# Growing the sums of seven block products in PSUM, with ScalarE copying partial sums: one step of a hybrid streaming encoder

## The chip, the core and the metric

The kernel runs on one core of a Trainium2 chip. TensorE multiplies matrices into PSUM (eight banks of 2 KB per partition), VectorE and ScalarE read PSUM and SBUF, GpSimd works in SBUF, and transfers between memory and SBUF are issued by SyncE. The metric is the device time of one launch in microseconds (us), shown as the median of three runs. In the profile PE is TensorE, PEld its loading of weights, DVE VectorE, ACT ScalarE, POOL GpSimd and SP SyncE.

## What is computed

One inference step of an encoder layer, for 4096 prompt tokens and 32 sample tokens of width 1024:

```
h    = RMSNorm_pre(x)
proj = h @ w_in      # [B_a | C_a | X_a | Z_a | qkv | Z_g | a_dec | b_beta]
y_a  = B_a * conv3_causal(C_a * X_a) * silu(Z_a)     # group A, 512 channels
y_g  = RMSNorm_head(gated_delta_rule(...)) * silu(Z_g)   # group B, 4 heads of 128
y    = x + RMSNorm_post(concat(y_a, y_g) @ w_out)
```

The outputs are y for both streams, and the last convolution inputs and recurrent states. The part that matters here is group A's four projections and the output projection.

## The kernel before, in words

Every fp32 operand of a large product is held as a pair of fp16 tiles (high and low part), and a product of two pairs takes three matmuls for each contraction tile (`mm3`, L863): high by high, high by low, low by high, over four contraction tiles, so twelve matmuls.

The kernel has three phases, which overlap at their borders. Phase 1 (up to about 1340 us of the span) works through group B in 16 blocks of 256 tokens, and prepares group A's weights beside it. Phase 2 (about 1343 to 2043 us) computes group A for eight blocks of 512 tokens; phase 3 (about 2043 us to the end) computes the output for 16 units of 256 tokens.

In phases 2 and 3 a product C = A B is computed by quarters, with seven products instead of eight (`winograd`, L869, after Strassen and Winograd). The sums of quarters of A and B are made beforehand: in `prep_a` (L659) and `h_load` (L886) for group A, in `mix_prep` (L1117) and `prep_out` (L1033) for the output. The loop over the seven products then sums their results into four quarters in SBUF, c11, c12, c21 and c22. With P0 to P6 in the order of that loop, c11 = P0 + P1, U2 = P0 + P2, U3 = U2 + P3, c12 = U2 + P4 + P5, c22 = U3 + P4, c21 = U3 + P6. The first product is copied out of PSUM by ScalarE (L877). The six others are added by VectorE to what lies in SBUF (L881): one addition for each, two for P4, so seven additions for each call.

Phase 2 calls `winograd` from `a_pairs` (L959): 64 calls, one for each block, each pair of channel tiles p = 0, 1 and each of the projections X, C, B and Z (g = 0 to 3, in this order), on quarters of 256 columns. Its seven products go two to a bank into four banks, of the tags "pj" and "g" in turn. After C, VectorE multiplies C by X (L976, two instructions of 512 columns). After Z, `conv_gate` (L944) does the causal convolution on VectorE (L946 to L951), multiplies it by B (L953), takes silu of Z on ScalarE (L955), and multiplies both on GpSimd (L957). The results of a call lie in two tiles of a ring of six (`dtile`, L857). Four calls take eight tiles, so the two tiles of Z are those of X, which the convolution uses as scratch until L953 has read them.

Beside these calls stands the preparation of the next block: `h_load` computes differences on GpSimd (L900 to L916), converts them on ScalarE (`put`, L896) and subtracts on GpSimd again (L897). `prep_out` converts w_out on ScalarE (L1053) and stores it by DMA through a ring of two tiles.

Phase 3 calls `winograd` once for each unit, from `out_unit` (L1167), on quarters of 512 columns. Each product has a bank of its own, of "pj" and "g" in turn (four banks). `norm_out` (L1145) squares the quarters on ScalarE (L1155), computes the inverse norm on VectorE (`rsqrt`, L112 to L119, and L1157 to L1160), scales on VectorE (L1163), adds the residual on GpSimd (L1164) and stores. `mix_prep` for the unit two ahead runs beside it: `token_scales` (L1087) takes absolute values on ScalarE (L1092), their sums on GpSimd (L1094) and one matmul into a bank of the tag "r" (L1089, L1095), scales the channels on VectorE (L1110), and the operands are made by ScalarE (L1128), VectorE (L1129) and GpSimd (L1135 to L1141). SBUF tiles of phase 3 come from a ring of 26 (`vtile`, L1081).

The order of instructions on each engine is not written out by hand: the framework orders them when the kernel is built, by priorities and a model of their times, so that products of neighbouring calls are interleaved. On the chip each engine runs its queue in that fixed order, and an instruction that waits holds back all behind it. A product that writes a bank waits until what was read from that bank has been read.

The banks are allotted by kind of use (L153): two each of "pj", "g" and "r", one each of "o" and "m".

Of the kernel before, what the change touches and what calls it, by code (L numbers as in the profile page):

```python
# [10 lines left out]
BF16 = mybir.dt.bfloat16  # L11
# [14 lines left out]
# Operands of the split products are scaled by powers of two: h (bounded by 32) by 2^HS, each  # L26
# column of the weights so that its sum of magnitudes lies in [2^WS, 2^(WS+1)). The sums that the
# Strassen-Winograd products take of them stay in the range of fp16, too.
# [4 lines left out]
NXT = 5  # buffers of the rows of x and of the weights in preparation  # L33
SG = 0  # the group of blocks that the sample goes with
LS = 2  # groups at the end whose products of q and k come a step earlier
XPE = 256  # tokens whose h is transposed on the tensor engine, the rest by DMA
AH = 1  # how far the preparation of weights runs ahead of the products, from step AS on
AS = 5
VLN = (20,)  # channel tiles of which the vector engine takes the scaling, or the low part
# [3 lines left out]
def bc(ap, axis, n):  # L43
    """ap with a new axis of n repeats."""
    shape = list(ap.shape)
    shape.insert(axis, n)
    return ap.unsqueeze(axis).to_broadcast(shape)
# [3 lines left out]
def hybrid_kernel(  # L51
# [24 lines left out]
    ident = const([P, P], F32, "ident")  # L76
    make_identity(nc, ident)
    tri = const([P, P], BF16, "tri")  # tri[k, i] = 1 where k <= i
# [3 lines left out]
    rev = const([P, P], BF16, "rev")  # rev[k, i] = 1 where k > i  # L82
    V.tensor_scalar(rev, tri, -1.0, 1.0, ALU.mult, ALU.add)
    # sums relative to the middle of a chunk; the last column gives its start
# [13 lines left out]
    mneg = const([P, P], F32, "mneg")  # mneg[j, i] = 0 where j <= i, else far below  # L98
# [5 lines left out]
    nea = const([P, NH], F32, "nea")  # -exp(a_log), all partitions  # L104
    dtb = const([P, NH], F32, "dtb")
    gwc = const([P, 1], F32, "gwc")
    usc = const([P, 32], F32, "usc")  # per channel tile: 1 / (scale of w * scale of h)
    ug = const([P, 8], F32, "ug")
    cw = const([P, 4, 12], F32, "cw")  # conv weights of qkv, unscaling folded in
    ca = const([P, 3, 4], F32, "ca")  # L110

    def rsqrt(x, y, t):  # L112
        """y = 1 / sqrt(x) for positive x, by Newton's iteration; t is scratch."""
# [8 lines left out]
    NB2P = SEQ // NB2  # L122
    # h of a block: (half of its rows, half of its tokens, high or low part, ...)
# [10 lines left out]
    # pairs of channel tiles of group A, in the order of their products: X, C, B, Z  # L134
    pairs = [(4 * g + 2 * p, p) for p in range(2) for g in (2, 1, 0, 3)]
    # channel tiles of group B in the order of their products
    b_order = [20, 21, 22, 23, 16, 17, 18, 19, 24, 25, 26, 27, 28, 29, 30, 31]

    def w_slot(i, shape, dtype, nm):
        """Room of 2 KB for a part of the weights."""  # L140
        return wp.tile(shape, dtype, tag=f"w{i}", name=f"w{i}_{nm}")
# [8 lines left out]
    # PSUM: the eight banks by kind of use  # L150
# [5 lines left out]
    # =================== phase 1: group B ===================  # L156
# [11 lines left out]
    def scaled(cts, n=P, urow=None):  # L168
        """Of the channel tiles of w_in (one or two): w * ln_pre with scaled columns, and the
        unscaling."""  # L170
# [4 lines left out]
        for i, ct in enumerate(cts):  # L175
            if 20 <= ct < 24:  # the first ones go to room that is not yet in use
                w = tl([P, D], F32, "v" if ct < 22 else "zg", 2, f"w{ct}")
            else:
                w = te([P, D], F32, "xt", NXT, f"w{ct}")
# [30 lines left out]
    # order of the activation tables: exponentials and silus are queued in turn  # L210
# [11 lines left out]
    def xprep(b):  # L222
        """h of the block, transposed, as an fp16 pair."""
# [8 lines left out]
        for i, t0 in enumerate(range(0, n, P)):  # L232
# [5 lines left out]
            else:  # a place that is not yet in use  # L238
# [33 lines left out]
    def gates(b):  # L272
        """Log-decays, their sums in the chunk, and the decays between its positions; by steps."""
# [26 lines left out]
        # u = 1 + e; log1p(e) = ln(u) + (e - (u - 1)) / u, sigmoid = 1 / u  # L300
# [14 lines left out]
        # the log-decays as three bf16 parts, whose sum they are  # L315
# [15 lines left out]
        # exponents: whole chunk, from here to its end, from its start to here; sum from the middle  # L331
# [22 lines left out]
    def in_turn(steps):  # L354
        """The steps of several blocks in turn."""
# [4 lines left out]
    def decays(b):  # L360
        """The decays between the positions of a chunk, and those to and from its ends."""
# [31 lines left out]
    def qkv_pair(b, c0, dst):  # L393
        """Channel tiles c0, c0+1 (of q, k, v): conv and silu into dst (P, 2, n)."""
# [20 lines left out]
    def stage1(b, c):  # L415
        """Chunk c: norms of q and k, products with k, decays."""
# [35 lines left out]
    def rnorms(b):  # L452
# [10 lines left out]
        V.tensor_tensor(br, b["beta"], rk, ALU.mult)                           # beta rk  # L463
        V.scalar_tensor_tensor(nb_, br, -1.0, rk, ALU.mult, ALU.mult)          # -b' = -beta rk^2
        V.tensor_tensor(nbe, nb_, b["e1"], ALU.mult)                           # -b' e^gb
        V.tensor_scalar(cc, rq, P ** -0.5, None, ALU.mult)                     # c = rq / sqrt(dk)
# [3 lines left out]
    def subst(b):  # L470
        """Inverses of the unit triangular 32x32 blocks on the diagonal: 32 blocks, of which lane
        (g, block) finds columns 8 g to 8 g + 7 by forward substitution."""
# [13 lines left out]
        # rows times beta / (|k|^2 + eps); |k|^2 is the block's diagonal  # L486
# [25 lines left out]
    # the inverse's transpose, for two chunks; its lower blocks stay zero  # L512
# [772 lines left out]
```

## Time and profile before

| what | value |
|---|---|
| median of 3 runs | 2450.47 us (2447.03 to 2458.69) |
| profiled execution, span | 2457.2 us |
| time around the span | not told by a view; the longest run, 2458.69 us, is 1.5 us above the span |
| busy shares over the span: PE, DVE, ACT, POOL | 88%, 77%, 43%, 53% |
| mean granted TensorE clock | 0.944 of 2.4 GHz |

The shares are means over three phases with different limits, so the rows below are taken by phase: a stretch of 583 us of phase 2 (1460 to 2043 us, where the border to phase 1 is past), and phase 3 (2043 to 2457 us). A row of a group gives the line, engine and operation, what is written and read, the shape, the count, and then the busy time and the mean duration of one; behind the second bar stands the idle time of the engine before these instructions, and what ended it.

### The profile page before, as it was taken

What the parts mean: (1) busy time and instruction counts of PE and PEld (TensorE: products, weight loads), DVE (VectorE), ACT (ScalarE), POOL (GpSimd) and SP (SyncE); (2) the same over time, 40 slices, a digit from 0 to 9 for tenths busy, and PEclk for the clock granted to TensorE, in tenths of its full rate; (3) what the DMA queues carried; (4) which work ended last, traced back from release to release, by engine and by line L of the source; (5) the groups of instructions that cost most, each with busy time, mean ns of one, the idle gap of its engine ahead of it and who ended that gap; (6) DMA issues with size and microseconds to landing.
All of it is one profiled execution on the core that took longest, in us unless ns stands there. A gap on an engine that the chain in (4) does not pass through costs nothing. (4 is left out here: it accounts for less than half of the span.)

```text
span 2457.2 us, 48833 instructions
## 1 busy us (share of the span) xinstructions
PE 2157.5 (88%) x18434; PEld 1704.9 (69%) x18434; DVE 1893.4 (77%) x4878; ACT 1046.3 (43%) x2617; POOL 1312.7 (53%) x1665
## 2 busy tenths in 40 slices
PE   3677999999999989999998799899989999888876
PEld 2565877778778777778877588787878885333332
DVE  3886879887678988668776766667684578899998
ACT  3454556555656556555653222122211133343432
POOL 3526356554464764175453724756754435556764
PEclk9888999999999999999988899999999999999988
DMA  5244343423423443233344042121121053233332
GB/s 113 53 102 92 78 94 88 113 70 85 128 73 85 111 96 110 48 100 78 68 125 148 14 175 98 50 99 57 61 82 53 10 190 107 92 116 116 121 124 86
DMA packets 301524, 227.69 MB, mean 93 GB/s; under 512 B 166904, under 2 KB 237368, under 8 KB 301288
## 3 DMA queue, kind: packets, MB, share of 16 engines
q1 hardware_dynamic: 301288, 224.58, 33.3%
q8 instruction: 144, 2.36, 0.4%
q14 instruction: 92, 0.75, 0.1%
HBM read 130.99 MB, written 77.79 MB: 85 GB/s over the span
## 5 line engine op out<-in xcount | busy, mean ns | idle before, releaser
L388 PE MATMUL pj_c<-hhi,w 128*128 128x256 f16 x1536 | 429.0, 279 | 1.2 <-DMA hhi<-xth 1.2
L390 PE MATMUL pj_c<-hhi,w 128*128 128x256 f16 x1536 | 428.8, 279 | 0.0
L389 PE MATMUL pj_c<-hlo,w 128*128 128x256 f16 x1536 | 428.7, 279 | 0.0
L867 PEld LDWEIGHTS <-w_a 128*128 128x128 f16 x2880 | 272.8, 100 | 65.7 <-issue 29.6
L495 POOL TENSOR_TENSOR la<-la,lt 128x1024 f32<-128x1024 f32 x16 | 38.7, 2421 | 459.2 <-DVE lt L490 274.8
L867 PEld LDWEIGHTS <-opm 128*128 128x128 f16 x1344 | 135.5, 102 | 212.1 <-issue 72.8
L500 POOL TENSOR_TENSOR lt<-lt 128x112 f32<-128x112 f32 (+29 forms) x496 | 251.0, 506 | 38.8
L390 PEld LDWEIGHTS <-w 128*128 128x128 f16 x2176 | 216.1, 101 | 59.8 <-POOL w L652 28.8
L499 POOL TENSOR_TENSOR lt<-la,lt 128x112 f32<-128x112 f32 (+29 forms) x496 | 231.8, 467 | 38.8
L388 PEld LDWEIGHTS <-w 128*128 128x128 f16 x2176 | 216.3, 101 | 34.7 <-issue 2.1
L389 PEld LDWEIGHTS <-w 128*128 128x128 f16 x2176 | 216.3, 101 | 31.1 <-issue 0.3
L405 DVE SCALAR_TENSOR_TENSOR qk<-u,cw,qk 128x256 f32<-128x256 f32 x384 | 215.0, 596 | 8.6 <-ACT qk L403 7.8
L867 PE MATMUL pja<-op,w_a 128*128 128x256 f16 x1536 | 197.2, 279 | 7.3 <-DVE w L881 4.1
L867 PE MATMUL pjo<-w_o,opm 128*128 128x512 f16 x672 | 170.4, 406 | 27.6 <-DVE v5c L881 5.2
L867 PE MATMUL go<-w_o,opm 128*128 128x512 f16 x672 | 162.4, 391 | 13.1 <-DVE v18c L881 2.8
L867 PE MATMUL ga<-op,w_a 128*128 128x256 f16 x1152 | 152.0, 278 | 15.3 <-DVE w L881 8.2
L388 PE MATMUL pj_z<-hhi,w 128*128 128x256 f16 x512 | 146.8, 287 | 0.0
L390 PE MATMUL pj_z<-hhi,w 128*128 128x256 f16 x512 | 146.7, 287 | 0.0
L389 PE MATMUL pj_z<-hlo,w 128*128 128x256 f16 x512 | 146.7, 287 | 0.0
L1094 POOL TENSOR_TENSOR mab<-mab 128x1024 bf16<-128x1024 bf16 (+2 forms) x48 | 82.1, 1711 | 73.2 <-ACT mab L1092 71.5
L1129 DVE TENSOR_TENSOR opm<-mx,opm 128x512 f16<-128x512 f32 x112 | 111.6, 1016 | 8.2 <-ACT opm L1128 8.2
L881 DVE TENSOR_TENSOR w<-pja,w 128x256 f32<-128x256 f32 x168 | 67.2, 419 | 59.9 <-PE pja L867 57.4
(849 smaller groups left out, 5264.2 us busy)
## 6 DMA issues: line engine op xcount, KB each, us to landing
xt<-in_x_prompt_dram SPq DMA_DIRECT2D x32, 512.0 KB
op<-hTd SPq DMA_DIRECT2D x32, 512.0 KB
mx<-mxd SPq DMA_DIRECT2D x16, 1024.0 KB
xtw<-in_w_in_dram SPq DMA_DIRECT2D x28, 512.0 KB
wad<-hl SPq DMA_DIRECT2D x56, 256.0 KB
gB<-gd SPq DMA_DIRECT2D x16, 516.0 KB
hTd<-hhi SPq DMA_DIRECT2D x16, 512.0 KB
hTd<-hlo SPq DMA_DIRECT2D x16, 512.0 KB
```

Of the source, the lines that this page charges most:

```text
L388: T.matmul(pt[:, i, :n], wh[:, k, :], b["hi"][:, k, :n], start=k == 0, stop=False)
L389: T.matmul(pt[:, i, :n], wh[:, k, :], b["lo"][:, k, :n], start=False, stop=False)
L390: T.matmul(pt[:, i, :n], wl[:, k, :], b["hi"][:, k, :n], start=False, stop=k == KT - 1)
L405: V.scalar_tensor_tensor(d, u[:, i, j:j + n], cw[:, j, c0 + i:c0 + i + 1], d, ALU.mult, ALU.add)
L495: E.tensor_tensor(la, la, bc(rl, 1, 32), ALU.mult)
L499: E.tensor_tensor(tm, bc(la[:, j, j + 1:32], 2, w), bc(lt[:, j, 0:w], 1, r), ALU.mult)
L500: last = E.tensor_tensor(lt[:, j + 1:32, 0:w], lt[:, j + 1:32, 0:w], tm, ALU.subtract)
L867: T.matmul(out, lt(x, k), rh(y, k), start=start and k == n == 0, stop=stop and k == 3 and n == 2)
L881: V.tensor_tensor(dst, p, src, ALU.add)
L1094: G.tensor_tensor(ab[:, 0:m], ab[:, 0:m], ab[:, m:2 * m], ALU.add)
L1129: V.tensor_tensor(mo[:, q, 1], src, mo[:, q, 0], ALU.subtract)
```

## The change

The seven sums grow in three PSUM banks X, Y and Z (tags "pj", "g" and "r"). The products are reordered so that X holds, one after the other, P0, then U2, then U3, then c21, by matmuls that add to what is there. Y holds one product, and Z the sum of two. ScalarE copies a bank's partial sum to SBUF at each point where it is needed. VectorE keeps two additions from PSUM (c11 and c12). One more addition, of two SBUF tiles (c22), is given to VectorE in group A and to GpSimd in the output. The last sum, c21, stays in PSUM for the caller: the C projection multiplies it from there, the others copy it on ScalarE. The order of operands follows the new order of products. `token_scales` takes its bank from the tag "m" in place of "r". Comments are removed throughout, which is left out here.

```diff
-    def mm3(out, lt, rh, start, stop):
+    def mm3(out, lt, rh, start, stop, more=False):
         for k in range(4):
             for n, (x, y) in enumerate(((0, 0), (0, 1), (1, 0))):
-                T.matmul(out, lt(x, k), rh(y, k), start=start and k == n == 0, stop=stop and k == 3 and n == 2)
+                T.matmul(out, lt(x, k), rh(y, k), start=start and k == n == 0, stop=stop and k == 3 and n == 2,
+                         skip_group_check=more)
-    def winograd(lts, rhs, ps, c11, c12, c21, c22):
-        for i, p in enumerate(ps):
-            mm3(p, lts[i], rhs[i], True, True)
-            if i == 0:
-                A.activation(c21, p, AF.Copy)
-            else:
-                for dst, src in (((c11, c21),), ((c12, c21),), ((c21, c12),), ((c12, c12), (c22, c21)),
-                                 ((c12, c12),), ((c21, c21),))[i - 1]:
-                    V.tensor_tensor(dst, p, src, ALU.add)
+    def winograd(lts, rhs, nm, n, c11, c12, u3, c22, E):
+        X, Y, Z = (bank(t, [P, n], f"{t}{nm}") for t in ("pj", "g", "r"))
+        def p(i, b, start):
+            mm3(b, lts[i], rhs[i], start, True, not start)
+        p(0, X, True)
+        A.activation(c11, X, AF.Copy)
+        p(1, Y, True)
+        V.tensor_tensor(c11, Y, c11, ALU.add)
+        p(2, X, False)
+        A.activation(c12, X, AF.Copy)
+        p(3, Z, True)
+        A.activation(c22, Z, AF.Copy)
+        p(4, X, False)
+        A.activation(u3, X, AF.Copy)
+        E.tensor_tensor(c22, c22, u3, ALU.add)
+        p(5, Z, False)
+        V.tensor_tensor(c12, Z, c12, ALU.add)
+        p(6, X, False)
+        return X
...
     def a_pairs(j, op, p):
...
-            ps = [bank("pgpg"[i] + "j" * (i % 2 == 0), [P, 2, NB1], f"a{nm}_{i}") for i in range(4)]
...
-            winograd([lambda x, k, q=q: w[q][:, x, k] for q in (0, 1, 4, 5, 3, 6, 2)],
-                     [lambda x, k, q=q: op[:, q, x, k] for q in (0, 2, 5, 4, 1, 3, 6)],
-                     [ps[i // 2][:, i % 2] for i in range(7)], ds[0][:, l], ds[0][:, h], ds[1][:, l], ds[1][:, h])
+            c21 = winograd([lambda x, k, q=q: w[q][:, x, k] for q in (0, 1, 4, 3, 5, 6, 2)],
+                           [lambda x, k, q=q: op[:, q, x, k] for q in (0, 2, 5, 1, 4, 3, 6)],
+                           f"a{nm}", NB1, ds[0][:, l], ds[0][:, h], ds[1][:, l], ds[1][:, h], V)
             got.append(ds)
             if g == 1:
-                for i in range(2):
-                    V.tensor_tensor(ds[i], ds[i], got[0][i], ALU.mult)
+                V.tensor_tensor(ds[1][:, l], c21, got[0][1][:, l], ALU.mult)
+                V.tensor_tensor(ds[0], ds[0], got[0][0], ALU.mult)
+                V.tensor_tensor(ds[1][:, h], ds[1][:, h], got[0][1][:, h], ALU.mult)
+            else:
+                A.activation(ds[1][:, l], c21, AF.Copy)
...
     def token_scales(nm, mx, n):
-        ap_ = bank("r", [P, NB1], f"am{nm}")[:, :n]
+        ap_ = bank("m", [P, NB1], f"am{nm}")[:, :n]
...
     def out_unit(u):
...
-        ps = [bank(("pj", "g")[(u + i) % 2], [P, 512], f"o{u}_{i}") for i in range(7)]
-        winograd([lambda x, k, q=q: mo[:, q, x, k] for q in range(7)],
-                 [lambda x, k, q=q: WO[q, k][:, x] for q in range(7)], ps, c11, c12, c21, c22)
+        order = (0, 1, 2, 4, 3, 5, 6)
+        x = winograd([lambda x, k, q=q: mo[:, q, x, k] for q in order],
+                     [lambda x, k, q=q: WO[q, k][:, x] for q in order], f"o{u}", 512, c11, c12, vtile(f"u3{u}"), c22, G)
+        A.activation(c21, x, AF.Copy)
```

## Rows read from the trace of the kernel before

**Rows 1.** Busy time by stretch: us, PE, PEld, DVE, ACT, POOL; clock, DMA share, GB/s.

```profile
1460.00:2043.00 583.00, 543.38 (x4955) 476.43 (x4954) 383.89 (x752) 119.86 (x236) 316.43 (x249) 0.98 0.25 86
2043.00:2457.00 414.00, 339.32 (x1472) 151.25 (x1469) 382.33 (x705) 158.13 (x346) 253.00 (x159) 0.92 0.34 109
...
1840.00:1880.00 40.00, 40.00 (x369) 35.85 (x367) 21.34 (x49) 5.66 (x11) 19.32 (x17) 1.00 0.04 14
```

**Rows 2.** What TensorE waited for, 1460 to 2043 us: total, times, longest.

```profile
PE ga L867 <- DVE d L881: 10.5, 4, 3.3
PE ga L867 <- DVE w L881: 8.5, 5, 2.9
PE pja L867 <- DVE w L881: 8.1, 10, 2.3
PE pja L867 <- DVE d L881: 5.4, 10, 1.5
PE pja L867 <- ACT w L877: 4.3, 2, 3.8
```

**Rows 3.** The chain that ended last, 2200 to 2260 us: start, us, what.

```profile
2225.74 2.53 DVE v21c L1163
...
2229.93 0.61 DVE v3c L881
2230.59 4.35 PE pjo L867 x12
```

**Rows 4.** VectorE's additions L881 alone, by stretch: us, DVE, clock, DMA share, GB/s.

```profile
1460.00:2043.00 583.00, 159.16 (x394) 0.98 0.25 86
2043.00:2457.00 414.00, 76.03 (x117) 0.92 0.34 109
```

**Rows 5.** ScalarE's copies L877: group, and one of phase 3 (timeline).

```profile
L877 ACT ACTIVATE w<-pja x38: 360/383/384, 1465.6 to 2037.6; 128x256 f32<-128x256 f32 x38
...
2231.35 0.58 ACT L877 ACTIVATE v11c<-go 128x512 f32<-128x512 f32 x1
```

**Rows 6.** Timeline, 2216 to 2230 us: start, us, instruction, idle time before.

```profile
2216.39 2.75 PE L867 MATMUL pjo<-w_o,opm 128*128 128x512 f16 x12
...
2218.98 2.75 PE L867 MATMUL go<-w_o,opm 128*128 128x512 f16 x12
...
2223.32 0.74 DVE L1163 SCALAR_TENSOR_TENSOR v19c<-v19c,oss,v26lnq 128x512 f32<-128x512 f32 x1
2223.48 1.71 POOL L1164 TENSOR_TENSOR v24x<-v20c,v24x 128x512 f32<-128x512 f32 x1 [2.14 <-DVE v20c L1163]
...
2223.98 1.76 DVE L1163 SCALAR_TENSOR_TENSOR v22c<-v22c,oss,v27lnq 128x512 f32<-128x512 f32 x1
...
2229.86 0.68 DVE L881 TENSOR_TENSOR v3c<-pjo,v3c 128x512 f32<-128x512 f32 x1
```

**Rows 7.** ScalarE's copies L877, 1460 to 2043 us: idle until (us, times).

```profile
  PE pja L867: 132.1, 30
  DVE w L953: 46.2, 7
  DVE d L953: 22.7, 5
```

**Rows 8.** What ScalarE waited for, 1460 to 2043 us.

```profile
ACT op L896 <- POOL tsc L902: 80.8, 22, 6.3
ACT op L896 <- POOL tsc L913: 38.0, 10, 4.1
ACT hl L1053 <- DMA wod<-hl: 36.5, 16, 5.8
...
ACT op L896 <- POOL tsc L916: 22.7, 9, 4.5
```

**Rows 9.** Clock beside a long stall, and beside short ones: us, PE, clock, DMA.

```profile
2229.00:2235.00 6.00, 4.41 (x13) 0.72 0.09 22
...
1640.00:1680.00 40.00, 37.77 (x344) 1.00 0.20 67
```

## The prediction

> **What bounds the kernel now.** The page gives TensorE 88% of the span and VectorE 77%, but these are means over phases, so I first read busy time by stretch. In phase 2 (583 us) TensorE issues 4955 matmuls. In a stretch where it is never idle, 369 of them take 40 us, 0.108 us each [rows 1], so the 4955 need 537 us and 46 us are lost. In phase 3 (414 us) VectorE is busy for 382 us, 92%, and TensorE for 339 [rows 1]. A product of twelve matmuls there takes 2.59 us from start to start [rows 6], so the seven of a unit take 18.1 us, and 16 units 290 us. So phase 2 is bound by TensorE with some holes, and phase 3 by VectorE.
>
> Next, what opens the holes. In phase 2 the waits of TensorE name VectorE's additions L881 four times, 10.5 + 8.5 + 8.1 + 5.4 = 32.5 us, and ScalarE's copy with 4.3 us [rows 2]. The rest of the 46 us are short gaps and time at a lower clock. In phase 3 the chain of waits goes along VectorE from one operation to the next and reaches TensorE only through an addition [rows 3]: the product that starts at 2230.59 us was released by an addition that stood in VectorE's queue behind a scaling. That product took 4.35 us where the earlier ones started 2.59 us apart [rows 3, 6], and the granted clock around it was 0.72 [rows 9]. So a long stall costs twice: the idle time, and a slower product after it.
>
> **The change, part by part.**
>
> *VectorE's additions, phase 3.* A unit goes from seven additions from PSUM to two, so 16 x 5 = 80 leave. In the chain such an addition takes 0.61 us from its start to the next step [rows 3], with 0.68 us of its own [rows 6]. At 0.60, 80 of them are 48 us. VectorE sets the end here, so this counts in full at first. Bounds: 0 if another engine takes over at once, 48 if none does.
>
> *The sum c22 on GpSimd, phase 3.* This is 16 additions of two SBUF tiles. The nearest row of that shape takes 1.71 us [rows 6], so 27 us on GpSimd, which goes from 253 to 280 us of 414 [rows 1]; it stays free enough. But the same scaling on VectorE, L1163, took 0.74 us once and 1.76 us beside that GpSimd addition, while an addition with one operand in PSUM kept to 0.68 [rows 6]. If each of the 16 stretches one such instruction of VectorE by 1.0 us, 16 us are given back; if none, 0. I take the middle, 8, since an addition finds VectorE sometimes at such an instruction and sometimes at one with an operand in PSUM. The Trainium skill (Perfetto Trace Analysis, Optimizing Scalar/DVE Operations) warns that GpSimd and VectorE share a read port, so that moving work between the two might not help. By it I would take the full 16 us and forecast 8 us more.
>
> *ScalarE's copies.* A call has five copies in place of one, four where C multiplies from PSUM: in phase 2 304 in place of 64, in phase 3 80 in place of 16. Each takes 0.38 us on 256 columns and 0.58 us on 512 [rows 5], so ScalarE gets 240 x 0.38 = 91 us in phase 2 (of which it was busy for 120 of 583) and 64 x 0.58 = 37 us in phase 3 (158 of 414) [rows 1]. It comes nowhere near a bound in the mean. What counts is when a copy happens. P2 may not write X before the copy of P0 is out, P3 not before that of P0 + P2, P6 not before that of U3, and P5 waits for Z in the same way. Between each pair lies one product on another bank: 12 x 0.108 = 1.30 us in phase 2, so 1.30 - 0.38 = 0.92 us of cover, and 2.59 - 0.58 = 2.0 us in phase 3. That is free while ScalarE is at hand, and if it is not, TensorE waits for the rest, unless the order has products of the next call to put in between (X, Y and Z have a second bank each).
>
> How often is it at hand? Of 56 copies in this stretch of phase 2, 30 found ScalarE waiting for the product, 12 waited for L953 [rows 7], and TensorE lost 4.3 us to ScalarE [rows 2]. In proportion, 240 more copies cost 4.3 x 240 / 56 = 18 us. Bounds: 0 if the cover holds everywhere. From above: ScalarE's queue stood 57 times at a conversion that waited for GpSimd or for a store, 178 us in all, 3.1 us each [rows 8]. If a needed copy stands behind each of them, each costs 3.1 - 0.9 = 2.2 us, 125 us in all. I take 18, from the row that is about this very copy. In phase 3, with twice the cover, I take 5.
>
> *The wait at Z.* The first copy of Z, now into c11, needs the tile that L953 of the first channel tile reads last; before, c21 needed the second one's, later by one L953. It remains a wait of ScalarE (12 times, 69 us [rows 7]). Behind it in the queue stand the conversions of `h_load` and `prep_out`, then GpSimd's subtractions; and TensorE at P2. Since VectorE loses additions ahead of L953, I expect the wait to shrink, and cost it at nothing beyond the 18.
>
> *VectorE's additions, phase 2.* 64 calls go from seven to three, so 256 leave, at 159.16 / 394 = 0.40 us [rows 4]: 103 us that were mostly not on the path. What they bring is fewer stalls: banks Y and Z have until the call after the next for VectorE's additions, where before TensorE stopped while VectorE was in a convolution. I take 20 of the 32.5 us; bounds 0 and 46, all the holes. The C projection gets one multiplication more (three for two), 16 x 0.4 us on VectorE, hidden in what it has just been relieved of; without that cover 6 us.
>
> *At nothing:* the other order of operands (h of the next block is made a block ahead; without that cover 1.3 us, one product, for each of eight blocks) and the bank "m" in place of "r" in `token_scales` (one matmul and one read for each unit; at worst a product's 2.59 us for each of 16 units). No DMA is moved.
>
> **Sum.** Phase 3: 48 - 8 - 5 = 35 us. Phase 2: 20 - 18 = 2 us. 2457.2 - 37 = 2420 us for an execution such as the profiled one, whose span lies 6.7 us above the median of 2450.47; against the median 2413 us, 1.5% faster. Its own range is 2395 to 2428.
>
> **Rivals.**
>
> *A, the copies hide everywhere.* All holes of phase 2 and all 48 us of phase 3: 2450 - 46 - 48 = 2356 us. For it speaks that ScalarE is busy for 21% and 38% of the two stretches [rows 1]; against it, that VectorE in phase 3 is not freed of GpSimd, and TensorE needs 290 us of full clock there at least.
>
> *B, phase 3 gets a new bound.* VectorE's 382 - 48 = 334 us meet TensorE's 339 [rows 1], part of which is at a low clock, and the two wait for each other through ScalarE. Half of the 35 us remain: 2450 - 18 = 2432 us.
>
> *C, it is hidden anyway.* The stalls move from the additions to the copies one for one: within 0.5%, 2450 us. The change does what it says in any case, since the additions are gone from the code; but it need not show.
>
> *D, slower.* ScalarE's queue becomes the place where TensorE stops in phase 2. If half of the 57 waits of [rows 8] stand ahead of a copy that TensorE needs, they cost 62 us against the 35 of phase 3, and the 20 of phase 2 are not had: 2450 + 62 - 35 = 2477 us. It decides the sign from about 16 of the 57 on. For it speaks that the queues' order is fixed beforehand, and that these waits show it to be wrong by 3 us at a time; against it, that only 4.3 us of such stalls show now [rows 2]. Beside it stands a rule of the Trainium skill (Perfetto Trace Analysis, Matmuls): independent groups of matmuls should rotate through the banks, so that the reading of one overlaps the next group. X takes four of seven products, which goes against it, though with a product on Y or Z between each two.
>
> Short stalls alone should not lower the clock: a stretch with 344 of 369 matmuls had 1.00 [rows 9].
>
> **Chances.** Forecast 0.45, A 0.12, B 0.15, C 0.09, D 0.19. About 0.5% is what a measurement of this kernel can tell from no change. Faster: 0.45 + 0.12 + 0.15 = 0.72; same 0.09; slower 0.19. The range leaves out D alone: from A's 2356 to 2456, which holds most of C.
>
> **What would show it.** In phase 2, waits of TensorE for L881 shrink from 32.5 us to some 12, and waits for ScalarE's copies stay under 25. In phase 3, VectorE's busy time falls from 382 us to about 345, the phase from 414 to about 380 us, and GpSimd gains about 27 us. The forecast is wrong if TensorE's waits for the copies exceed some 50 us (D), if VectorE falls as said and the phase does not get shorter (B), or if the holes of phase 2 close altogether (A).

## The result, and the profile after

The changed kernel takes 2486.51 us (median of 4 runs, 2484.88 to 2489.97), the kernel before 2452.15 us beside it. The ratio is 1.014 with a 95% interval of 1.0117 to 1.0163: slower by 34 us. The forecast was 2413 us, in a range that ended at 2456. The direction was wrong.

The first part of the page after the change:

```profile
span 2486.1 us, 48743 instructions
PE 2162.3 (87%) x18434; PEld 1708.3 (69%) x18434; DVE 1793.2 (72%) x4558; ACT 1158.0 (47%) x2921; POOL 1339.8 (54%) x1681
```

VectorE's share fell from 77% to 72% and ScalarE's rose from 43% to 47%, as meant. The time did not follow. To find where, I cut both traces at the same points of work: the first matmul of group A's products, the 336th (four calls), the 5040th of 5376, and the last one of the output. From the 5040th on, group A's last calls and the output overlap; this is called the last stretch below. What lies behind it, up to the end, is 14 us before and 13 after. Busy time in the three stretches, before (columns: us, then busy time of PE, PEld, DVE, ACT, POOL with the number of instructions; granted clock, DMA share, GB/s):

```profile
1343.00:1420.00 77.00, 62.67 (x527) 49.53 (x524) 57.26 (x122) 19.74 (x58) 53.57 (x69) 0.87 0.11 31
1420.00:2007.00 587.00, 546.83 (x4984) 480.34 (x4983) 391.10 (x785) 122.16 (x253) 317.82 (x251) 0.98 0.25 86
2007.00:2443.00 436.00, 375.16 (x1800) 183.23 (x1798) 393.90 (x725) 163.98 (x360) 255.17 (x161) 0.93 0.35 112
```

and after:

```profile
1341.00:1432.00 91.00, 72.30 (x583) 62.86 (x581) 61.03 (x151) 30.00 (x96) 59.46 (x74) 0.79 0.13 36
1432.00:2005.00 573.00, 535.94 (x4906) 471.42 (x4905) 285.75 (x481) 174.22 (x407) 290.10 (x230) 0.97 0.25 84
2005.00:2473.00 468.00, 383.62 (x1805) 184.28 (x1804) 397.73 (x686) 212.35 (x468) 305.26 (x194) 0.91 0.33 107
```

The border to phase 1 is 14 us longer, the bulk of group A 14 us shorter, and the last stretch 32 us longer. The border after the change also holds 68 more of phase 1's own matmuls, which stand in the bulk before, so the two are best taken together: 664 us in both. In the bulk VectorE lost 105 us of work, and TensorE gained nothing by it. In the last stretch VectorE is as busy as before (398 against 394 us), in spite of the additions from PSUM that left (25 us of them in place of 87), and in a longer time. More preparation of output units stands in it: 112 operand subtractions take 123 us there, where 98 took 96.

Each stretch is from one execution, so small differences say little. Phase 1, with the same 11141 matmuls ahead of group A's first in all twenty traces, took from 1328 to 1344 us. A kernel with the order of the one before (*before_m*, below) has 433 us in the last stretch in place of 436, and 660 us ahead of it in place of 664.

What TensorE waited for in phase 2 after the change, 1460 to 2044 us (in total, times, longest):

```profile
PE pjpja L868 <- DVE w L990: 14.8, 5, 5.9
PE pjpja L868 <- ACT w L884: 6.9, 3, 3.8
PE pjpja L868 <- DVE d L990: 3.9, 2, 3.2
PE pjpja L868 <- ACT d L884: 3.3, 3, 1.7
```

The 32.5 us for additions [rows 2] are down to 1.4. In their place stand 18.7 us for L990, the multiplication of C by X that reads c21 in bank X, and ScalarE's copies (18.2 us over all rows of the view from 1440 to 2000 us).

In the last stretch the waits before began with these (2007 to 2443 us):

```profile
PE oip L1106 <- DVE me L1101: 17.5, 6, 4.5
PE pjo L867 <- DVE v5c L881: 5.2, 1, 5.2
PE pjo L867 <- DVE v24c L881: 4.3, 1, 4.3
```

and after (2005 to 2473 us):

```profile
PE oip L1124 <- DVE me L1119: 30.1, 8, 8.0
PE pjpjo L868 <- DVE opm L1147: 21.9, 7, 6.0
PE pjpjo L868 <- ACT v9c L888: 5.3, 1, 5.3
PE pjpjo L868 <- ACT v25c L1191: 5.2, 1, 5.2
```

Summed by kind, the additions L881 cost TensorE 41 us in 20 waits before. After, they cost 1. But the copies cost 21 us in 10 waits, VectorE's late operands (L1147, L1129 before) 24 in 9 where there were none, ScalarE's half of the operands (L1146) 4 in 3, and the small matmuls of the next units' preparation 34.5 in place of 19. One such stall in the timeline after (start, us, instruction, idle time before it):

```profile
2342.41 0.75 DVE L1181 SCALAR_TENSOR_TENSOR v9c<-v9c,oss,v27lnq 128x512 f32<-128x512 f32 x1
...
2343.74 1.75 DVE L1181 SCALAR_TENSOR_TENSOR v11c<-v11c,oss,v27lnq 128x512 f32<-128x512 f32 x1
2344.66 0.57 ACT L888 ACTIVATE v18c<-pjpjo 128x512 f32<-128x512 f32 x1
2345.41 1.75 DVE L1181 SCALAR_TENSOR_TENSOR v10c<-v10c,oss,v26lnq 128x512 f32<-128x512 f32 x1
2347.08 3.41 DVE L1147 TENSOR_TENSOR opm<-mx,opm 128x512 f16<-128x512 f32 x2
2348.89 7.57 PE L868 MATMUL pjpjo<-w_o,opm 128*128 128x512 f16 x22 [6.02 <-DVE opm L1147]
2350.42 0.68 DVE L895 TENSOR_TENSOR v18c<-rro,v18c 128x512 f32<-128x512 f32 x1
2351.13 0.72 ACT L1173 ACTIVATE jk<-v18c,iv 128x512 bf16<-128x512 f32 x1 [5.90 <-DVE v18c L895]
2356.05 0.60 ACT L892 ACTIVATE v21u<-pjpjo 128x512 f32<-128x512 f32 x1 [4.11 <-PE pjpjo L868]
```

VectorE does the norm of one unit (L1181) ahead of the operands of the next (L1147). TensorE waits 6.02 us for them, and ScalarE stands 5.90 us at a square for an addition behind them in VectorE's queue. VectorE has no gap here, but it works on another unit than the one TensorE waits for; over the last stretch it is busy for 398 of 468 us.

### The profile page after: what moved, and what is told of

Read it like the earlier page. It is cut to its first block, busy times and chain, and to the rows that moved or that the text cites. A ratio compares the mean times of both kernels' runs of the same rounds, so it can differ in the third digit from the quotient of the medians.

```text
span 2486.1 us, 48743 instructions
## 1 busy us (share of the span) xinstructions
PE 2162.3 (87%) x18434; PEld 1708.3 (69%) x18434; DVE 1793.2 (72%) x4558; ACT 1158.0 (47%) x2921; POOL 1339.8 (54%) x1681
## 4 chain that ended last, share of the span: by engine, by line
DVE 30%; PE 27%; POOL 19%; DMA 11%; issue 6%; ACT 5%; SPq 2%; DVEq 0%; POOLq 0%; ACTq 0%
PE pjpja L868 7%; POOL lt L499 5%; POOL lt L500 5%; DVE qk L405 3%; DVE opm L1147 3%; PE rra L868 3%; DMA xtw<-in_w_in_dram 2%; PE gq L442 2%; DMA mx<-mxd 2%; PE gga L868 1%; PE pj_c L388 1%; PE pj_c L390 1%; PE pj_c L389 1%; DMA gB<-gd 1%; PE pj_z L388 1%
## 5 line engine op out<-in xcount | busy, mean ns | idle before, releaser
L868 PE MATMUL pjpjo<-w_o,opm 128*128 128x512 f16 x768 | 200.5, 414 | 45.8 <-DVE opm L1147 21.9
L868 PE MATMUL pjpja<-op,w_a 128*128 128x256 f16 x1536 | 193.4, 277 | 16.4 <-DVE w L990 4.2
L1147 DVE TENSOR_TENSOR opm<-mx,opm 128x512 f16<-128x512 f32 x112 | 123.3, 1116 | 41.9 <-ACT opm L1146 41.7
L1146 ACT ACTIVATE opm<-mx 128x512 f16<-128x512 f32 x112 | 67.0, 622 | 86.5 <-DVE mx L1128 31.3
L406 ACT ACTIVATE qk<-qk 128x512 f32<-128x512 f32 x64 | 39.9, 628 | 138.1 <-DVE qk L405 138.0
L868 PE MATMUL rra<-op,w_a 128*128 128x256 f16 x768 | 99.6, 275 | 0.1
```

The costliest lines, as they stand in the source:

```text
L406: queued("silu", lambda: A.activation(dst, dst, AF.Silu))
L868: T.matmul(out, lt(x, k), rh(y, k), start=start and k == n == 0, stop=stop and k == 3 and n == 2, skip_group_check=more)
L1146: A.activation(mo[:, q, 0], src, AF.Copy)
L1147: V.tensor_tensor(mo[:, q, 1], src, mo[:, q, 0], ALU.subtract)
```

## The experiments

Each kernel ran beside the kernel before on the same chip, and ratios are to that. The chips differ between groups of runs (the kernel before took 2446 to 2453 us), so kernels of different groups are compared by ratios. Durations of stretches are cut as above, one execution each.

### Which half of the change costs it

*a_only* has group A's new form and the old output (bank "r" in `token_scales`); *out_only* the reverse; *out_c22_dve* is the changed kernel with the output's c22 addition on VectorE; *before_m* is the kernel before with the other bank.

```diff
-... f"o{u}", 512, c11, c12, vtile(f"u3{u}"), c22, G)
+... f"o{u}", 512, c11, c12, vtile(f"u3{u}"), c22, V)      # out_c22_dve
-        ap_ = bank("r", [P, NB1], f"am{nm}")[:, :n]
+        ap_ = bank("m", [P, NB1], f"am{nm}")[:, :n]       # before_m
```

> Group A in the new form, the output (and the bank of token_scales) as before. Theory T, the loss comes from the new form in the output phase alone, where ScalarE's copies stand in one queue with the squares and the operand conversions: 2452 us, within 8 us of the kernel before, since group A alone broke even in the two traces. Rival R1, the new form in group A delays the preparation of the first output units, so that the output phase starts with less done: 2465 to 2475 us, half or more of the loss of 34 us.

> Group A as before, the output in the new form. Theory T: 2486 us, within 8 us of the changed kernel. Rival R1: 2455 to 2468 us, since the preparation of the first units then runs as in the kernel before.

> The changed kernel, but the sum c22 of the output on VectorE in place of GpSimd. Rival R2, GpSimd's additional instruction and what it stretches on VectorE is the cause: 2455 to 2468 us. Theory T: 2475 to 2490 us, since 16 additions on VectorE cost some 10 to 16 us and the stretched ones give about as much back.

> The kernel before, with token_scales in the single bank m in place of a bank of r, and nothing else. Rival R3, the single bank holds up the preparation of the units: over 2465 us. Theory T: 2452 us, within 5 us.

| kernel | us | ratio | 95% interval |
|---|---|---|---|
| a_only | 2482.36 | 1.0136 | 1.0099 to 1.0174 |
| out_only | 2468.06 | 1.0088 | 1.0053 to 1.0122 |
| out_c22_dve | 2485.48 | 1.0153 | 1.0122 to 1.0185 |
| before_m | 2451.21 | 1.0013 | 0.9992 to 1.0034 |

Either half loses, and together they lose less than their sum: 33 and 22 us by the ratios, against 34. Neither theory held for both halves: a_only lies above the range of either, and out_only at the upper end of R1's. GpSimd's share and the bank "m" make no difference. In a_only the last stretch is 453 us against 436. In out_only it is 449, with VectorE relieved by 28 us. Of the last stretch alone the two losses, 17 and 13 us, nearly make the 32 of the changed kernel. a_only, then out_only:

```profile
2009.00:2462.00 453.00, 384.21 (x1807) 184.20 (x1805) 409.96 (x753) 180.29 (x402) 270.06 (x177) 0.91 0.33 109
2003.00:2452.00 449.00, 371.59 (x1770) 179.25 (x1768) 365.56 (x643) 194.68 (x423) 278.52 (x177) 0.91 0.33 108
```

### Late preparation

In a_only the output's code is that of before, yet its last stretch is 17 us longer. One thing that differs is when the first units are prepared. The scales' first matmul of `token_scales` before (instruction, durations in ns, first and last start):

```profile
L1095 PE MATMUL ram<-mab,ones x4: 270/272/273, 1783.2 to 2045.6; 128*128 128x256 bf16 x4
```

and after:

```profile
L1113 PE MATMUL mam<-mab,ones x4: 269/272/273, 2000.0 to 2083.6; 128*128 128x256 bf16 x4
```

In a_only the first of these starts at 2004.1 us. The work that filled TensorE's holes in phase 2 now comes up to 217 us later. *a_hoist* puts it earlier for two units; *a_hoist_border* also gives the first two calls of `a_pairs` the old form.

```diff
+        if j in (5, 6):
+            mix_scale(j - (5, 6)[0])          # load and token_scales of unit 0, 1
         if j > 1:
             a_pairs(j, ops[j], 0)
```

> Group A new, output as before, and the scaling of the first two output units written two blocks and one block earlier in the program (before the products of blocks 5 and 6), so that TensorE's small matmul for it stands earlier in its queue. Theory R1a, group A alone loses because its queue no longer has holes into which the order of instructions puts that scaling, so that VectorE has two more units to scale in the output phase: 2455 to 2468 us, 14 us or more below the 2482 us of group A alone. Rival B, the loss sits at the border to phase 1, where Z's bank is also that of the recurrence: 2476 to 2485 us, no change.

> As the one before, and the first eight calls of group A (blocks 0 and 1, first pairs), which run beside the end of phase 1, in the old form with banks pj and g alone. Rival B: 12 to 18 us below the kernel with the earlier scaling. Theory R1a alone: within 6 us of it.

a_hoist took 2478.83 us (1.0109, 1.0081 to 1.0138), a_hoist_border 2481.77 (1.0114, 1.0089 to 1.0139). Neither gave back what was expected. With the units hoisted the last stretch was still 459 us, with 392 us of VectorE's work, as before:

```profile
2001.00:2460.00 459.00, 378.65 (x1807) 181.79 (x1805) 391.69 (x730) 171.82 (x384) 258.49 (x164) 0.93 0.32 107
```

So neither the amount of VectorE's work nor the lateness of these two units explains the loss. With the old form at the border as well, the time up to product 5040 went from 673 us to 664, that of the kernel before, and the last stretch stayed at 458. The border is taken up again below.

### ScalarE's squares, and the small matmuls

The four nosq kernels leave out ScalarE's squares (L1155 before, L1173 after) and take a constant for the sum of squares. VectorE then computes the norm's scale from that constant, so with the squares its wait for them is left out too.

```diff
...
-                A.activation(jk, cs[hf], AF.Square, scale=iv[:, t:t + 1], accum_out=...)
+        G.memset(ss[:, 0], 1.0)
```

> Group A as before, output in the new form, without ScalarE's squares of the output (the norm's sum is a constant). Theory T2, in the output phase ScalarE's fixed queue holds copies and conversions behind squares that wait for VectorE's additions: the excess of 18 us over the kernel before falls to 6 us or less against the old form without squares. Rival, the copies themselves or the banks cost it: the excess stays at 12 us or more.

> The kernel before without ScalarE's squares of the output (the norm's sum is a constant): the other half of the pair. 2425 to 2445 us by either theory, since VectorE keeps its 382 us less the waits for the squares.

> Group A in its new form, the output in its old form, and the squares of norm_out left out (the sums of squares are a constant, so y is scaled wrongly). Theory T2 (ScalarE's fixed queue: squares that wait for VectorE's additions hold back conversions and copies): without the squares group A's new form costs little in the output phase either, so the time is at most 10 us over the 2445 us of the kernel before without squares (2440 to 2455), where with squares it was 32 us over. Theory T4 (the preparation of the first output units comes late, and the output phase never catches up, squares or not): the excess stays near 30 us, 2470 to 2478.

> The changed kernel without the squares of norm_out (as above). T2: at most 10 us over the kernel before without squares (2440 to 2455), against 34 us with them. T4 (late preparation, independent of the squares): 2470 to 2480. If both halves add up as they do with squares, it is the sum of what the two halves cost without squares, the output's half being -4 us.

| kernel | us | ratio | 95% interval |
|---|---|---|---|
| before_nosq | 2444.90 | 0.9959 | 0.9939 to 0.9979 |
| out_nosq | 2440.42 | 0.9951 | 0.9921 to 0.9980 |
| a_nosq | 2468.18 | 1.0053 | 1.0032 to 1.0074 |
| after_nosq | 2462.70 | 1.0047 | 1.0035 to 1.0059 |

The output's new form alone loses nothing where there are no squares: 2440 against 2445 us. The changed kernel's loss falls from 34 us to 22 (1.0047 against 0.9959), group A's only from 33 to 23. So the output form loses only where there are squares, and group A's form without them too. a_nosq and after_nosq lie between the ranges of the two theories.

The last stretches say it more plainly. In the output's old form they are as long with the squares as without: 436 and 436 us in the kernel before, 453 and 453 in a_only. In the new form they are 449 and 428 us in out_only, and 468 and 451 in the changed kernel. before_nosq, then out_nosq, where VectorE has 27 us less to do and 8 us are gained:

```profile
1988.00:2424.00 436.00, 373.65 (x1793) 182.38 (x1792) 398.37 (x724) 114.96 (x230) 251.66 (x179) 0.94 0.35 113
2003.00:2431.00 428.00, 366.41 (x1771) 178.52 (x1770) 370.95 (x645) 147.38 (x295) 286.46 (x195) 0.94 0.35 115
```

How the squares act is less clear. ScalarE stood 118 us in 28 waits at squares before (all rows of its waits, 2007 to 2443 us), and 84 us in 24 after. Before, one copy for each unit shared that queue; now five do. If the waits themselves did the harm, a norm emitted one unit later should help:

```diff
+        while pending:
+            pending.pop()()             # norm_out of the unit before
...
-            norm_out(f"{u}", ((c11, c12), (c21, c22)), ...)
+            pending.append(lambda: norm_out(f"{u}", ((c11, c12), (c21, c22)), ...))
+            if u + 2 == NU2:
+                pending.pop()()
             return
```

> The changed kernel with norm_out of each output unit emitted one unit later, behind the products of the next unit, so that its squares stand in ScalarE's queue when the additions they read are long done. Nothing is left out. T2: copies and conversions are no longer held back by squares, and the time falls below the changed kernel's 2486.5 by 20 us or more (2445 to 2466). T4: 2475 to 2490. A loss (over 2490) would say that the delayed norms collide at the end of the program or with the tiles of the ring.

> The kernel before with the same delayed norm. Control for the run above: T2 says that the squares cost the kernel before as well (leaving them out gave 7 us), so at most that is to be had: 2443 to 2452. If the delay by itself costs time at the end of the program, it shows here: 2455 to 2470.

after_late took 2482.61 us (1.0139, 1.0116 to 1.0162), before_late 2455.84 (1.0016, 0.9999 to 1.0033). The waits at squares fell only to 68 us in 12, and nothing was gained in all: the last stretch was 460 us in place of 468, but phase 2 and the end behind the last stretch took as much more. That the output form's loss needs the squares is shown. That it comes through these waits is not, and a part of it may be the order of the queues, which every one of these edits changes.

The largest single row of TensorE's waits, for the small matmuls that turn the scales (L1124), was tried in both kernels by moving them behind the unit's products:

```diff
-        ip = bank("o", [P, 2], f"ip{nm}")           # in token_scales
...
+        iv = turn(f"{u}", er, NB1)                  # in out_unit, behind winograd
```

> The changed kernel, with the small matmuls that turn the scales (ip) and the copy behind them taken out of token_scales and put behind the unit's products, just ahead of norm_out. Theory T7 (these small matmuls stand in TensorE's queue and wait for VectorE's late scales, 27.1 us in seven waits in the output phase, with all products behind them): the time falls by 12 to 27 us, to 2459 to 2475. T7 wrong (the products behind them would wait for the same late operands anyway): within 6 us of 2486.

> The kernel before with the same move. T7: 19.0 us in seven such waits there, so 8 to 19 us less: 2431 to 2442. T7 wrong: within 6 us of 2450. If the move helps here as much as in the changed kernel, it says nothing of the change, only that these waits are real cost in both.

after_ip took 2475.87 us (1.0124, 1.0094 to 1.0154), before_ip 2461.96 (1.0066, 1.0042 to 1.0089). The first is within the error of the changed kernel's ratio, and the second lost 16 us where 8 to 19 were to be won. In neither kernel was the wait that the row names won back.

### A border, behind which the queues are equal

The order on each engine is made when the kernel is built, so any edit moves it everywhere. To take this out, *before_fence* and *a_fence* hold the preparation of units 0 and 1 behind group A's last instructions. Behind group A, TensorE's last 1475 matmuls and VectorE's last 769 instructions are the same in the same order in both traces, and ScalarE's and GpSimd's differ by the place of one each at the start.

```diff
-            mix_prep(0)
-            mix_prep(1)
...
+    with tc.issue_after(done["V"]), tc.issue_after(done["A"]):
+        mix_prep(0)
+        mix_prep(1)
     out_conv_a("p", hists[-1], nca_p)
```

> The kernel before, with the preparation of output units 0 and 1 held behind the last group-A unit's instructions on VectorE and ScalarE (a border between the phases). Reference for the next run; the overlap of the phases is lost, which costs the preparation of one unit, an estimate of 15 to 40 us: 2465 to 2490.

> Group A in its new form, the output in its old form, with the same border. Behind the border every engine's queue (TensorE, VectorE, ScalarE, GpSimd) holds the output phase's instructions in the very order of the run above. Theory T6 (group A's new form costs nothing by itself; its holes in TensorE's queue are gone from the build-time model, so preparation falls behind and the output phase gets a worse fixed order): equal to the run above within 5 us. Theory T8 (the new form itself costs time, by ScalarE's copies or by work left over at its end): 15 to 32 us above it, as without the border.

before_fence took 2481.99 us (1.0149, 1.0121 to 1.0178), a_fence 2496.25 (1.0203, 1.0168 to 1.0238), 14 us more. That is between what the two theories said (within 5 us, or 15 to 32), and the stretches tell why. before_fence:

```profile
1341.00:1417.00 76.00, 60.86 (x520) 48.77 (x517) 56.59 (x121) 19.60 (x58) 54.01 (x69) 0.89 0.11 29
1417.00:1983.00 566.00, 535.09 (x4975) 474.43 (x4973) 362.51 (x724) 102.53 (x207) 288.90 (x231) 0.99 0.26 87
1983.00:2466.00 483.00, 386.64 (x1810) 186.94 (x1807) 420.43 (x783) 181.03 (x405) 296.24 (x181) 0.89 0.31 104
```

a_fence:

```profile
1342.00:1433.00 91.00, 72.60 (x586) 63.45 (x584) 59.75 (x150) 29.88 (x96) 59.40 (x74) 0.81 0.13 36
1433.00:2000.00 567.00, 533.23 (x4892) 469.75 (x4890) 277.03 (x469) 167.28 (x390) 282.68 (x226) 0.97 0.25 84
2000.00:2483.00 483.00, 385.19 (x1817) 187.38 (x1814) 415.97 (x767) 187.16 (x421) 295.97 (x181) 0.89 0.32 104
```

With equal queues the last stretch is equal, 483 and 483 us. So the 17 us that a_only loses there come from the order, with the preparation that moved into the stretch, and not from anything that group A's new form does to the output. What is left, 17 us, lies before product 5040 (641.6 and 658.8 us before rounding, with 5481 matmuls in both). The border to phase 1 takes 15 us of it, but it now also holds 68 more of phase 1's own matmuls, which before_fence has in the bulk. The granted clock there, before the change (us, PE busy, clock, DMA share, GB/s):

```profile
1360.00:1380.00 20.00, 13.44 (x103) 0.87 0.13 25
1380.00:1400.00 20.00, 19.98 (x175) 0.79 0.06 4
```

and after:

```profile
1360.00:1380.00 20.00, 9.86 (x55) 0.61 0.18 27
1380.00:1400.00 20.00, 14.79 (x117) 0.50 0.05 14
```

TensorE idles for half of 20 us, at small matmuls of phase 1 that wait for VectorE and for a DMA (6.6 us in all from 1355 to 1400 us), without group A's products between them, and then runs 20 us at 0.50 of full clock. *a_border_cx* undoes two parts of a_fence's group A: the first two calls are in the old form, and C's last sum is copied to SBUF before it is multiplied.

```diff
-            if g == 1:
-                V.tensor_tensor(ds[1][:, l], c21, got[0][1][:, l], ALU.mult)
-                V.tensor_tensor(ds[0], ds[0], got[0][0], ALU.mult)
-                V.tensor_tensor(ds[1][:, h], ds[1][:, h], got[0][1][:, h], ALU.mult)
...
+            elif g == 1:
+                A.activation(ds[1][:, l], c21, AF.Copy)
+                for i in range(2):
+                    V.tensor_tensor(ds[i], ds[i], got[0][i], ALU.mult)
```

> a_fence with two parts of group A undone, each read in its own stretch: (1) the first two calls of a_pairs, beside the end of phase 1, in the old form; (2) C's last sum copied out of PSUM by ScalarE as in the other projections, and multiplied by X from SBUF in two full instructions. The theory that group A's new form loses its 17 us at the border to phase 1 (chains of phase 1 stand bare in TensorE's queue, and the granted clock falls to 0.50 in 20 us) and in waits for the C times X multiplication that reads the bank (14.1 us) says: the first 336 products take 77 us again (91 in a_fence), those waits are gone, and up to product 5040 it takes 642 to 650 us against 658.9 in a_fence and 641.6 with the old form. If only the border counts: 650 to 654. If neither: over 655. The output phase has the same instructions in another order than a_fence, so its length is no test of this; the theory that order alone moves it by some 10 us would show as a length other than a_fence's 482 us.

It took 2492.01 us (1.0170, 1.0139 to 1.0201). Its stretches:

```profile
1335.00:1412.00 77.00, 61.29 (x517) 48.99 (x516) 56.26 (x121) 19.69 (x58) 53.60 (x70) 0.89 0.10 28
1412.00:1975.00 563.00, 533.94 (x4967) 473.22 (x4966) 291.79 (x516) 170.44 (x413) 292.13 (x231) 1.00 0.26 87
1975.00:2468.00 493.00, 382.59 (x1810) 184.82 (x1809) 420.13 (x766) 188.37 (x420) 280.91 (x181) 0.89 0.31 102
```

Up to product 5040 it needs 640 us, against 659 in a_fence and 642 in before_fence: the two parts together hold the whole loss of group A's form. How it divides between them isn't told, since phase 1's matmuls change place between the two stretches. At the border it also stays open whether the copies make the loss, or the banks of the tag "r", which the new form takes for Z and phase 1 uses too. No row of TensorE's waits there names the multiplication any more. The last stretch has the instructions of a_fence, but for C's copies and multiplications, in another order and takes 493 us in place of 483: order alone is worth some 10 us.

Last, *before_z* asks whether VectorE's quantity of work sets the old output phase. Two of the output's products grow in one bank, so an addition leaves and no copy comes.

```diff
+        for i, q in enumerate((0, 1, 2, 3, 4, 6, 5)):
+            p = ps[min(i, 5)] if q != 5 else ps[4]
+            mm3(p, ..., q != 5, True, q == 5)
...
```

> The kernel before, whose output products P4 and P5 grow in one bank (order P0, P1, P2, P3, P4, P6, P5): six additions on VectorE in place of seven for each unit, no more copies on ScalarE. The theory that VectorE's work sets the pace of the old output phase (394 us busy of 435) says up to 16 x 0.67 us = 11 us less: 2436 to 2446. The theory that the fixed order of the queues decides says anything from 2440 to 2465, as other small changes of order gave.

It took 2453.53 us (1.0020, 1.0001 to 1.0039). Its last stretch:

```profile
1997.00:2433.00 436.00, 374.75 (x1799) 181.51 (x1797) 382.38 (x705) 164.27 (x356) 256.27 (x161) 0.94 0.34 112
```

VectorE has 11.5 us less to do there than before (382.4 for 393.9), and the stretch is 436 us in both. The edit also changes the order, which is worth as much as the 11.5 us, so this run alone does not exclude that VectorE's work counts for a part; it adds to out_only and a_hoist. None of the fourteen kernels with the full computation beats the kernel before.

## Why the prediction was wrong, point by point

**"VectorE sets the end here, so this counts in full at first."** This step failed. It took 92% busy and a chain along VectorE [rows 1, 3] for a bound by quantity. The additions did leave: VectorE had 76.03 us of them [rows 4] and keeps 22.5. Of the 48 us none reached the end. In out_only VectorE has 28 us less to do in the last stretch, and it is 13 us longer; a_hoist has VectorE's work of before and takes 459 us there in place of 436; before_z takes 11.5 us from VectorE, gives them to no other engine, and gains nothing. Without the squares 27 us less work brought 8 us. What sets the phase in place of VectorE's quantity is shown in part: the order of the queues (483 or 493 us behind the border) and, for the output's new form, the squares. That four queues of fixed order wait for one another fits all of this, but the waits were not followed through.

**"In phase 3, with twice the cover, I take 5" for ScalarE's copies.** They cost TensorE 21 us in 10 waits. The cover of 2.0 us between products was right for a ScalarE that is at hand. But one that stands 5.90 us at a square is not. The squares were never weighed in the prediction, though their waits on VectorE were in the trace of before, 118 us of them; without squares the output's form costs nothing (out_nosq). That they act by holding up copies was not shown.

**Contention of GpSimd, 8 us.** The row-level effect is there: L1181 takes 0.75 or 1.75 us, as L1163 did [rows 6], and the 98 operand subtractions grew from 96.0 to 110.2 us in all. But moving c22 back to VectorE changes nothing (out_c22_dve, 2485.48 against 2486.51 us). The Trainium skill (Perfetto Trace Analysis, Optimizing Scalar/DVE Operations) warns that moving work between these two engines might not help, since they share a read port; these durations and out_c22_dve agree with it. No run shows the 8 us of the sum, or the 16, as a price in the time.

**Phase 2, "20 - 18 = 2 us".** The total to product 5040 is 664 us in both, so the sum looks right, and for a wrong reason. The copies' 18 us are what was measured, 18.2. The 20 us from fewer stalls did not come: the waits for additions went (32.5 us), but the C times X multiplication, which I put at nothing or 6 us, holds bank X until VectorE reaches it, 18.7 us. The border to phase 1, for which there was no term, takes 14 us more, with 68 more matmuls in it. Preparation that left phase 2 hid these losses; behind a border, before_fence and a_fence show them bare, 17 us. The Trainium skill (Perfetto Trace Analysis, Matmuls) asks for independent groups to rotate through the banks. The trace shows no price of going against it with X: TensorE's waits for the readers of X came to 36.9 us in phase 2, and its waits at the banks that rotate, in the kernel before, to 36.8 [rows 2].

**What was missing altogether** is that filling TensorE's holes changes the order made at build time. The first units' preparation had stood in phase 2 and came up to 217 us later. The last stretch of a_only took 17 us more, with the output's code of before.

**The rivals.** D (2477 us) gave nearly the time, but that was luck, for it had the wrong place: TensorE's stalls at ScalarE in phase 2 stayed at the 18 us of the forecast, and the loss lies in phase 3. C's "stalls move from the additions to the copies one for one" is what phase 2 shows, 36.8 us against 36.9, with the multiplication beside the copies. B was right that the three engines would wait for each other in phase 3; it put at half the gain what took all of it and more. Of the signs named ahead, those of phase 2 went as said or further (TensorE's waits for the additions 1.4 us, for the copies 18.2) and those of phase 3 did not: VectorE's busy time was to fall to 345 us and the phase from 414 to 380; it fell to 373 and the phase grew to 443:

```profile
2043.00:2486.00 443.00, 350.00 (x1512) 154.81 (x1511) 372.95 (x657) 197.52 (x435) 286.82 (x181) 0.90 0.33 107
```

**What stays open.** In the whole time the halves' losses don't add up (33 and 22 us make 34). What the new form costs by itself was told apart from what the order costs for group A alone; an output in the new form behind the same border was not tried, so its loss beside the squares may be a matter of order too. Why one order is worse than another was not traced instruction by instruction.

## What to carry to other kernels

A busy share of 92% does not show that an engine's quantity of work is the bound: take work from it without giving any to others, and see whether the time moves (before_z tried this, with less work than the order is worth). Before work is moved to an idle engine, read what stands in that engine's queue and waits for the engine that is being relieved. Where the order is made at build time, an edit also reshuffles everything behind it, here by some 10 to 17 us, so compare variants behind a border after which the queues are equal, and judge nothing smaller without one.

## What was not expected of the hardware

After 20 us in which TensorE was busy for 9.86 us, at a granted clock of 0.61, it was granted 0.50 for the next 20 us (1.2 of 2.4 GHz) while it was busy for 14.79; in the kernel before, 13.44 us busy were followed by 0.79. In group A's bulk waits of several microseconds show in the clock as well. In a_fence the mean was 0.97, and it was 0.83 in the 20 us with the longest wait for the multiplication, 5.9 us (1620 to 1640 us), and in the 20 us with a wait of 3.8 us for a copy (1540 to 1560 us). In a_border_cx, where the waits for the multiplication are gone, the mean was 1.00, and 0.92 in the 20 us with a wait of 4.8 us for a copy (1520 to 1540 us). The prediction expected this of a long stall in phase 3 [rows 9] and not of phase 2.
